# Sums of squares on ScalarE, and the first loads and conversions pinned in order of need, in a one-core hybrid encoder layer

## The chip, the cores and the metric

The kernel runs on 1 core of one Trainium2 chip. The metric is the device time of one execution in microseconds (us). An execution has five engines that run their own instruction queues: PE (TensorE, matmuls), DVE (VectorE), ACT (ScalarE), POOL (GpSimd) and SP (SyncE, which issues most of the DMAs). A difference of under 0.5% is about what a measurement of this kernel cannot tell from none.

## The reference

One encoder layer on 256 tokens of width 1024, all in float32. What matters here is its beginning:

```python
h = _rmsnorm(x, g_mix)                      # x * rsqrt(mean(x*x) + 1e-6) * g
rq, rk, rv, rg, nq, nk, nv, xq, gates = jnp.split(h @ w_in, split_points, axis=-1)
mem_n = _rmsnorm(mem, g_mem)                # 256 memory tokens of width 1024
mk, mv = jnp.split(mem_n @ w_mem_kv, 2, axis=-1)
...
lg_f = jax.nn.log_sigmoid(ret_decay_fwd)    # 4 heads; the same for bwd
...
x = x + (g_ret * y_ret + g_na * y_na + g_xa * y_xa) @ w_out
x = x + _hierarchical_moe(_rmsnorm(x, g_ffn), ...)   # 16 experts, 100 MB of weights
return _rmsnorm(x, g_final)
```

`nv`, `xq`, `nq` are 512 columns each of `h @ w_in` (values and queries of the neighbourhood attention, queries of the attention to the memory); `mk` and `mv` are the memory's keys and values.

## The kernel before, in words

**Products in three passes.** Every float32 product is made of three fp32r matmuls: each operand is split into a high part and the rest, and high x high, rest x high and high x rest are summed in PSUM (L261 to L263, L278 to L280 and L294 to L296). So a weight needs two steps before PE may use it: ACT casts the raw tile to its high part (`conv`, L126), DVE subtracts that from the raw tile (L127). A `unit` is one load of 1 MiB (L119) and two such conversions. Four raw tiles (`raw_tags`) and five tiles for the split halves (`hl_tags`) go round, so a load waits for the DVE of an earlier unit and a cast for the PE of an earlier unit.

**The norm is applied late.** The matmuls run on `x` times the gain only (`gained`, L235 and L237: ACT makes the high part, DVE the rest). The factor 1/rms of each token is worked out beside them: `squares` (L205 to L212) squares and sums the transposed tokens on POOL in eight instructions, `tokens` (L214 to L223) sums over partitions with two tiny matmuls into a PSUM tile (L219), DVE adds the epsilon (L221), POOL raises to the power -0.5 (L222). That gives `col`, one factor per token on the partition axis. `row_of` (L225 to L231) turns it into a row, by two DVE multiplications into the tile of the squares (L227), a matmul against ones (L228) and a copy from PSUM (L230). `pair_T` and `pair_N` multiply a result by the row or the column and split it.

**The order of the start.** A hand-ordered block (L243 to L263) first runs 17 transposes on PE, then, for each quarter `q` of the 1024 rows, `squares`, `gained`, the weight conversions (L256, L257) and 12 matmuls of `nv`, 48 in all, of 512 columns each. Then `tokens` for x, and `xq`, the row of x, `nq`, the memory's gains and squares, `tokens` for the memory, `mk`, the memory's row and `mv`, in this order on PE. `xq`, `nq` and `mk` are 96 matmuls of 256 columns each, `mv` 48 of 512. Outside of the hand-ordered blocks a scheduler sets the order on each engine by its own costs; an instruction in `keep_in_program_order` stays where the program has it. Each engine takes its instructions strictly in the order that results.

**Later.** The retention's decays come in by a load of 8 numbers (L385), and a chain of small DVE instructions works out their log-sigmoid (L421 to L439). Then attention, retention, the gates, the output product, and from about 330 us the 16 experts, whose weights are read straight from HBM.

Of the kernel before, what the change touches and what calls it, by code (L numbers as in the profile page):

```python
# [30 lines left out]
def hybrid_encoder_kernel(  # L31
# [101 lines left out]

# [70 lines left out]

    def squares(src, sq, q, pin=lambda i: i):  # L205
        dst = slice(2, 4) if q else slice(0, 2)
        ks = slice(2 * q, 2 * q + 2)
        pin(G.tensor_tensor(sq[:, dst], src[:, ks], src[:, ks], op=ALU.mult))
        if q:
            pin(G.tensor_tensor(sq[:, :2], sq[:, :2], sq[:, 2:4], op=ALU.add))  # L210
        if q == 3:
            pin(G.tensor_tensor(sq[:, 0], sq[:, 0], sq[:, 1], op=ALU.add))  # L212

    def tokens(sq):  # L214
        ones_f = tmp([P, P])
# [5 lines left out]
        V.tensor_scalar(col, pt[:, 2, :2], 1.0 / D, 1e-6, op0=ALU.mult, op1=ALU.add)  # L221
        tc.keep_in_program_order(G.tensor_tensor(col, col, nhalf[:, :2], op=ALU.pow))  # L222
        return col, pt, ones_f  # L223

    def row_of(tag, sq, col, pt, ones_f):  # L225
# [157 lines left out]
    mv_hi, mv_lo = pair_N("C1", proj_N(units(w_mem_kv[0], 512, D), memT_hi, memT_lo), col_m)  # L383
# [1013 lines left out]
```

## Time and profile before

| what | value |
|---|---|
| median of 3 runs | 555.55 us (554.69 to 557.27) |
| the profiled execution, its own time | 555.26 us |
| its span, first to last instruction | 553.4 us |
| PE busy | 533.1 us, 96% |
| DVE busy | 271.6 us, 49% |
| ACT busy | 225.7 us, 41% |
| POOL busy | 53.5 us, 10% |
| moved by DMA | 158.87 MB, mean 287 GB/s |

The span is 1.86 us shorter than the execution's own time. A line of the windows view gives, for a stretch of the span, each engine's busy time and number of instructions, the granted TensorE clock (1.00 is full), the DMA engines' busy share and their GB/s. A line of the timeline is one instruction, or several alike that follow each other (xN): start, duration, engine, line, operation, what it writes and reads, and in brackets how long its engine sat idle before it and what ended that. A matmul's duration is longer than the distance to the next one, since matmuls overlap; how fast PE goes is read from the distance between starts.

### The profile page before, as it was taken

The numbers are of one execution on the slowest core, as the hardware profiler recorded it, in microseconds if no ns is written. First come the engines' busy times: TensorE is split into PE (matmuls) and PEld (weight loads), VectorE is DVE, ScalarE is ACT, GpSimd is POOL, SyncE is SP. The second block draws the span as 40 slices with busy tenths as digits, with TensorE's granted clock in tenths as the row PEclk, the third lists the DMA queues.
The fourth block names the chain that finished last, engine by engine and source line by source line (L and its number), as shares of the span: only waits on it lengthen the run. The fifth ranks groups of instructions, "written<-read, shape, count | busy, mean of one in ns | idle before, by whom it ended". The sixth has DMA issues, their size and how long they took to land.

```text
span 553.4 us, 7530 instructions
## 1 busy us (share of the span) xinstructions
PE 533.1 (96%) x2916; PEld 363.6 (66%) x2916; DVE 271.6 (49%) x462; ACT 225.7 (41%) x372; POOL 53.5 (10%) x61
## 2 busy tenths in 40 slices
PE   8898999999999999999999999999999999999990
PEld 6798899987778888888888863353435343533440
DVE  6989759997647758565466271030112101211122
ACT  6653455877674555545435251121111111211132
POOL 5246601030000040000000000000000000000000
PEclk9899999999999999999999999999999999999996
DMA  8973998144443699648994598999999999999942
GB/s 290 386 238 113 226 262 208 54 152 153 152 146 125 202 346 349 216 152 324 374 345 172 218 366 319 417 406 415 408 415 408 410 411 408 416 405 416 407 172 81
DMA packets 80969, 158.87 MB, mean 287 GB/s; under 512 B 4496, under 2 KB 18864, under 8 KB 80928
## 3 DMA queue, kind: packets, MB, share of 16 engines
q1 hardware_dynamic: 79152, 154.68, 75.6%
q0 software_dynamic: 1488, 3.60, 3.7%
q8 instruction: 25, 0.41, 0.3%
q14 instruction: 16, 0.13, 0.1%
q10 hardware_dynamic: 288, 0.05, 0.0%
HBM read 157.27 MB, written 1.05 MB: 286 GB/s over the span
## 4 chain that ended last, share of the span: by engine, by line
PE 90%; POOL 2%; issue 2%; DVE 1%; DMA 1%; ACT 1%; SPq 0%; ACTq 0%
PE b L1163 20%; PE pj L294 9%; PE pj L295 9%; PE pj L296 9%; PE b L1182 9%; PE b L1095 3%; PE pj L278 3%; PE pj L280 3%; PE pj L279 3%; PE pj L1220 3%; PE at L330 1%; PE pj L846 1%; PE pj L848 1%; PE pj L847 1%; PE b L1193 1%
## 5 line engine op out<-in xcount | busy, mean ns | idle before, releaser
L127 DVE TENSOR_TENSOR h<-r,h 128x1024 fp32r<-128x1024 f32 x58 | 73.1, 1269 | 32.5 <-ACT h L126 32.1
L126 ACT CAST h<-r 128x1024 fp32r<-128x1024 f32 x58 | 59.9, 1048 | 26.8 <-PE pj L296 12.3
L294 PE MATMUL pj<-h,A 128*128 128x512 f32 x160 | 63.1, 394 | 0.0
L295 PE MATMUL pj<-h,A 128*128 128x512 f32 x160 | 62.5, 391 | 0.0
L296 PE MATMUL pj<-h,A 128*128 128x512 f32 x160 | 62.4, 390 | 0.0
L1171 DVE TENSOR_TENSOR gs<-gs,b 64x512 f32<-64x512 f32 x16 | 11.1, 691 | 87.1 <-ACT gs L1170 87.1
L278 PE MATMUL pj<-A,h 128*128 128x256 f32 x160 | 45.6, 285 | 0.0
L280 PE MATMUL pj<-A,h 128*128 128x256 f32 x160 | 45.5, 284 | 0.0
L279 PE MATMUL pj<-A,h 128*128 128x256 f32 x160 | 45.4, 284 | 0.0
L294 PEld LDWEIGHTS pj<-h,A 128*128 128x128 f32 x160 | 30.0, 188 | 7.1 <-issue 0.8
L296 PEld LDWEIGHTS pj<-h,A 128*128 128x128 f32 x160 | 30.0, 188 | 6.7 <-issue 0.4
L295 PEld LDWEIGHTS pj<-h,A 128*128 128x128 f32 x160 | 30.1, 188 | 6.2 <-DVE h L127 0.4
L1202 DVE SCALAR_TENSOR_TENSOR os<-b,c,os 128x512 fp32r<-128x512 f32 x16 | 12.0, 750 | 42.2 <-ACT os L1201 41.4
L280 PEld LDWEIGHTS pj<-A,h 128*128 128x128 f32 x160 | 30.7, 192 | 0.1
L279 PEld LDWEIGHTS pj<-A,h 128*128 128x128 f32 x160 | 30.7, 192 | 0.0
L278 PEld LDWEIGHTS pj<-A,h 128*128 128x128 f32 x160 | 30.7, 192 | 0.0
L1170 ACT ACTIVATE gs<-b 64x512 f32<-64x512 f32 x16 | 9.4, 589 | 51.8 <-PE b L1163 51.8
L1201 ACT ACTIVATE os<-b,c 128x512 fp32r<-128x512 f32 x16 | 11.0, 688 | 40.9 <-PE b L1182 39.9
L127 DVE TENSOR_TENSOR h<-G,h 128x1024 fp32r<-128x1024 f32 x18 | 22.0, 1232 | 7.1 <-ACT h L126 6.9
L1163 PE MATMUL b<-h,C 128*64 128x512 f32 x104 | 24.0, 592 | 0.0
L126 ACT CAST h<-G 128x1024 fp32r<-128x1024 f32 x18 | 18.9, 1049 | 11.5 <-PE pj L296 9.0
L1244 POOL TENSOR_TENSOR rstd<-var,nhalf 128x1 f32<-128x1 f32 x2 | 1.1, 542 | 219.2 <-DVE var L1243 219.2
(342 smaller groups left out, 1106.7 us busy)
## 6 DMA issues: line engine op xcount, KB each, us to landing
r<-in_w_in_dram SPq DMA_DIRECT2D x21, 1024.0 KB, 5.2
h<-in_w_exp_down_dram SPq DMA_DIRECT2D x10, 1024.0 KB, 11.5
h<-in_w_exp_gate_dram SPq DMA_DIRECT2D x13, 512.0 KB, 10.9
h<-in_w_exp_up_dram SPq DMA_DIRECT2D x13, 512.0 KB, 11.0
r<-in_w_exp_down_dram SPq DMA_DIRECT2D x6, 1024.0 KB, 11.4
G<-in_w_in_dram SPq DMA_DIRECT2D x5, 1024.0 KB, 9.5
A<-in_w_exp_down_dram SPq DMA_DIRECT2D x5, 1024.0 KB, 11.4
r<-in_w_exp_gate_dram SPq DMA_DIRECT2D x9, 512.0 KB, 10.2
```

What stands on the lines that cost most here:

```text
L126: A.copy(hi, part)
L127: V.tensor_sub(lo, part, hi.bitcast(F32))
L278: PE.matmul(pt, whi[:, cs], thi[:, k], start=k == 0, stop=False)
L279: PE.matmul(pt, whi[:, cs], tlo[:, k], start=False, stop=False)
L280: PE.matmul(pt, wlo[:, cs], thi[:, k], start=False, stop=k == kn - 1)
L294: PE.matmul(pts[a], thi[:, kk, ts], whi, start=first, stop=False)
L295: PE.matmul(pts[a], thi[:, kk, ts], wlo, start=False, stop=False)
L296: PE.matmul(pts[a], tlo[:, kk, ts], whi, start=False, stop=last)
L1095: PE.matmul(pts[u][:, j], x[:, a, ks], pd[:, a].rearrange("p e s -> p (e s)"), start=first and j + a == 0, stop=not first and j + a == 2,)
L1163: PE.matmul(pt[c * 64 : c * 64 + 64], xg[:, k, p % 2 * 2 + i], w[:, 2 * c + j], start=k == 0, stop=k == KT - 1)
L1182: PE.matmul(pts[n][i * 64 : i * 64 + 64], hh[:, 2 * u + k], ws[i][1][:, k, ns], start=u + k == 0, stop=u + k == 2)
L1220: PE.matmul(acc[a][n], q[:, a * P : (a + 1) * P], os[n][:, i], start=False, stop=last and i == 1)
```

## The change

The sums of squares leave POOL. For x, a second copy of x in its natural layout (1 MiB, tokens on partitions) is loaded after the weights of `xq`; ACT squares it and sums along the row in the same instruction (`accum_out`), which gives the per-token sum without a matmul. For the memory, ACT squares the transposed tokens in two instructions, POOL adds the pieces in three (1024, 512 and 256 columns), and the two tiny matmuls stand between the two halves of `mk` (`mid`), not ahead of it. `col` and row keep their form, but the multiplications of the row write a tile of their own, and the ones are made once. The weights of `xq` are loaded in four pieces in place of two; those of `nq`, `mk` and `mv` are converted at places that the program fixes. The decays are loaded at the very start, on ACT's DMA queue, and four DVE instructions that stood where the scheduler put them (the two multiplications of the rotary tables, and the two that read the decays) are pinned.

```diff
+    dec = cp.tile([P, 8], F32, name="dec")
+    A.dma_start(dec, decay.partition_broadcast(P))
...
-        pin(G.tensor_tensor(sq[:, dst], src[:, ks], src[:, ks], op=ALU.mult))
-        if q:
-            pin(G.tensor_tensor(sq[:, :2], sq[:, :2], sq[:, 2:4], op=ALU.add))
-        if q == 3:
-            pin(G.tensor_tensor(sq[:, 0], sq[:, 0], sq[:, 1], op=ALU.add))
+    def squares(src, sq):
+        pin = tc.keep_in_program_order
+        for h in range(2):
+            ks = slice(4 * h, 4 * h + 4)
+            pin(A.activation(sq[:, ks], src[:, ks], AF.Square))
+        for n in (4, 2, 1):
+            pin(G.tensor_tensor(sq[:, :n], sq[:, :n], sq[:, n : 2 * n], op=ALU.add))
...
+    def diag_of(col):
+        diag = tmp([P, T])
         for a in range(2):
-            V.tensor_scalar_mul(sq[:, 1, a * P : (a + 1) * P], ident, col[:, a : a + 1])
-        PE.matmul(pt[:, 0], ones_f, sq[:, 1], start=True, stop=True)
+            tc.keep_in_program_order(V.tensor_scalar_mul(diag[:, a * P : (a + 1) * P], ident, col[:, a : a + 1]))
+        return diag
...
-            squares(xT, sq, q)
             gained(xT, 0, hT_hi, hT_lo, ks)
...
-    col_x, *mean_x = tokens(sq)
...
+    xq_u = units_T(W, C_XQ, D, parts=2)
+    x_n = slot("F", [P, 2, D])
+    nc.sync.dma_start(x_n, x[0].rearrange("(a p) d -> p a d", p=P))
+    ms = tiny(2, tag="ms")
+    for a in range(2):
+        tc.keep_in_program_order(A.activation(x_n[:, a], x_n[:, a], AF.Square, accum_out=ms[:, a : a + 1]))
+    col_x = tiny(2, tag="col")
+    tc.keep_in_program_order(V.tensor_scalar(col_x, ms, 1.0 / D, 1e-6, op0=ALU.mult, op1=ALU.add))
+    power(col_x)
...
-    pts = proj_T(units_T(W, C_XQ, D), hT_hi, hT_lo)
-    row_x = row_of("q", sq, col_x, *mean_x)
+    pts = proj_T(xq_u, hT_hi, hT_lo)
+    nq_u = units_T(W, C_NQ, D, pin)
+    row_x = row_of("q", diag_of(col_x))
...
-    gained(memT, 1, memT_hi, memT_lo, range(KT))
+    pts = proj_T(nq_u, hT_hi, hT_lo)
+    gained(memT, 1, memT_hi, memT_lo, range(KT), pin)
     sq = slot("E1", [P, KT, T])
-    for q in range(4):
-        squares(memT, sq, q, tc.keep_in_program_order)
-    nq_hi, nq_lo = pair_T("E0", proj_T(units_T(W, C_NQ, D), hT_hi, hT_lo), row_x)
-    col_m, *mean_m = tokens(sq)
-    pts = proj_T(units_T(w_mem_kv[0], 0, D), memT_hi, memT_lo)
-    row_m = row_of("gs", sq, col_m, *mean_m)
+    mk_u = [unit(w_mem_kv[0][:, :256], 256, pin=pin)]
+    squares(memT, sq)
+    mk_u.append(unit(w_mem_kv[0][:, 256:512], 256, pin=pin))
+    nq_hi, nq_lo = pair_T("E0", pts, row_x)
+    cols = []
+    pts = proj_T(mk_u, memT_hi, memT_lo, lambda: cols.append(tokens(sq)))
+    (col_m,) = cols
+    diag_m = diag_of(col_m)
+    mv_u = units(w_mem_kv[0], 512, D, pin)
+    row_m = row_of("gs", diag_m)
...
-    dec = cp.tile([P, 8], F32, name="dec")
-    nc.sync.dma_start(dec, decay.partition_broadcast(P))
...
-    V.tensor_mul(cos, cos, row_x)
-    V.tensor_mul(sin, sin, row_x)
+    pin(V.tensor_mul(cos, cos, row_x))
+    pin(V.tensor_mul(sin, sin, row_x))
...
-    V.tensor_scalar_mul(e8, dec, -1.0)
+    pin(V.tensor_scalar_mul(e8, dec, -1.0))
...
-    V.tensor_scalar_min(lg, dec, 0.0)
+    pin(V.tensor_scalar_min(lg, dec, 0.0))
```

Three places show what moves. First, ACT between the conversions of `xq` (h on r and G of `w_in`) and the rows of the memory. Before (G_30 is the memory, E_17 a half of `nv`, h_35 to h_39 are the halves of `nq`):

```order
L126 CAST h_23_247<-G_21_242 128x1024
L235 ACTIVATE B_31_364<-G_30_362,gt 128x256 x5
L365 ACTIVATE E_17_231<-pj_127,col_228 128x512
L235 ACTIVATE B_31_364<-G_30_362,gt 128x256 x3
L126 CAST h_35_393<-r_34_391 128x1024
L126 CAST h_36_396<-r_34_391 128x1024
L126 CAST h_38_401<-r_37_399 128x1024
L126 CAST h_39_404<-r_37_399 128x1024
L126 CAST h_49_524<-r_48_522 128x1024
L301 CAST C_27_353<-t_28_354 128x512
```

Of the change (F_236 is x in its natural layout, h_26 to h_30 are the halves of `nq`, h_44 the first of `mk`):

```order
L126 CAST h_18_233<-G_16_227 128x1024
L380 ACTIVATE F_236,ms_238<-F_236 128x1024 x2
L386 ACTIVATE E_22_244<-pj_131,col_241 128x512
L126 CAST h_26_347<-r_25_345 128x1024
L126 CAST h_27_350<-r_25_345 128x1024
L126 CAST h_29_355<-r_28_353 128x1024
L126 CAST h_30_358<-r_28_353 128x1024
L313 CAST C_34_368<-t_35_369 128x512
L313 CAST C_34_368<-t_36_373 128x512
L246 ACTIVATE B_38_379<-G_37_377,gt 128x256 x8
L126 CAST h_44_498<-r_43_496 128x1024
L126 CAST h_45_501<-r_43_496 128x1024
```

The squares of x and the power behind them now stand ahead of the conversions of `nq`, and the eight gains of the memory have gone behind the split of `xq` (C_34).

Second, POOL at the memory's sums. Before (E_33 are the squares, G_30 is the memory):

```order
L208 TENSOR_TENSOR E_33_382<-G_30_362 128x512 x2
L210 TENSOR_TENSOR E_33_382<-E_33_382 128x512
L208 TENSOR_TENSOR E_33_382<-G_30_362 128x512
L210 TENSOR_TENSOR E_33_382<-E_33_382 128x512
L208 TENSOR_TENSOR E_33_382<-G_30_362 128x512
L210 TENSOR_TENSOR E_33_382<-E_33_382 128x512
L212 TENSOR_TENSOR E_33_382<-E_33_382 128x256
L222 TENSOR_TENSOR col_519<-col_519,nhalf 128x2
```

Of the change, POOL's whole start from the power of x on:

```order
L218 TENSOR_TENSOR col_241<-col_241,nhalf 128x2
L215 TENSOR_TENSOR E_42_495<-E_42_495 128x1024
L215 TENSOR_TENSOR E_42_495<-E_42_495 128x512
L215 TENSOR_TENSOR E_42_495<-E_42_495 128x256
L218 TENSOR_TENSOR col_579<-col_579,nhalf 128x2
```

The multiplications are gone from POOL, for x all of it but the power; the additions for the memory are left.

Third, DVE where the decays' chain begins. Before (t_43 is the first half of `nq`, h_52 and h_53 are halves of `mk`; 21 more of the chain follow, mixed with the next conversions):

```order
L127 TENSOR_TENSOR h_52_532<-G_51_530,h_52_532 128x1024
L302 TENSOR_TENSOR E_42_505<-t_43_506,E_42_505 128x512
L421 TENSOR_SCALAR e_71_730<-dec 128x8
L438 TENSOR_SCALAR lg<-dec 128x8
L422 TENSOR_TENSOR e_71_730<-e_71_730,dec 128x8
L425 TENSOR_SCALAR den_734<-e_71_730 128x8
L426 RECIPROCAL den_734<-den_734 128x8
```

Of the change (C_70 is the second half of `mv`, G_71 holds the cosines and sines, mx_772 belongs to the first softmax over the memory):

```order
L317 SCALAR_TENSOR_TENSOR C_70_712<-pj_663,col_579,C_70_712 128x512
L418 TENSOR_TENSOR G_71_717<-G_71_717,row_366 128x256
L419 TENSOR_TENSOR G_71_717<-G_71_717,row_366 128x256
L446 TENSOR_SCALAR e_73_724<-dec 128x8
L349 TENSOR_REDUCE mx_772<-at_759 128x4
L447 TENSOR_TENSOR e_73_724<-e_73_724,dec 128x8
L127 TENSOR_TENSOR h_110_997<-r_109_995,h_110_997 128x1024
L450 TENSOR_SCALAR den_728<-e_73_724 128x8
L350 TENSOR_SCALAR mx_772<-mx_772 128x4
L451 RECIPROCAL den_728<-den_728 128x8
```

The chain and the two multiplications of the tables by the row stand nine conversions later, inside the first softmax.

## Rows read from the trace of the kernel before

**Rows 1.** The page's first line: the span.

```profile
span 553.4 us, 7530 instructions
```

**Rows 2.** Windows: busy us (instructions) of each engine, PE clock, DMA share, GB/s.

```profile
5.30:22.90 17.60, 14.65 (x51) 10.45 (x51) 17.11 (x19) 12.47 (x22) 8.90 (x7) 0.90 1.05 370
16.80:20.10 3.30, 3.30 (x9) 2.56 (x8) 3.30 (x6) 2.14 (x3) 0.00 (x0) 0.51 1.09 387
34.80:46.80 12.00, 12.00 (x99) 11.75 (x97) 11.91 (x11) 5.00 (x6) 10.96 (x7) 1.00 0.42 126
73.40:85.00 11.60, 11.60 (x99) 11.60 (x98) 5.99 (x8) 7.59 (x17) 0.00 (x0) 1.00 0.86 275
85.00:125.00 40.00, 40.00 (x304) 36.69 (x303) 39.33 (x69) 28.21 (x56) 8.01 (x8) 1.00 0.48 133
300.00:540.00 240.00, 238.83 (x1243) 110.88 (x1242) 50.37 (x121) 50.08 (x97) 1.12 (x2) 1.00 0.96 374
```

**Rows 3.** Timeline, 11 to 24 us: start us, us, engine, what, [idle before].

```profile
11.58 2.69 DVE L237 SCALAR_TENSOR_TENSOR A<-E,gt,A 128x256 fp32r<-128x256 f32 x2
...
12.40 1.15 ACT L256 CAST h<-r 128x512 fp32r<-128x512 f32 x2
...
12.74 0.39 PE L261 MATMUL pj<-h,A 128*128 128x512 f32 x1
...
14.19 2.89 DVE L257 TENSOR_TENSOR h<-r,h 128x512 fp32r<-128x512 f32 x2
...
15.99 0.50 PE L263 MATMUL pj<-h,A 128*128 128x512 f32 x1 [2.34 <-DVE h L257]
...
17.01 0.87 DVE L237 SCALAR_TENSOR_TENSOR A<-E,gt,A 128x256 fp32r<-128x256 f32 x2
...
17.80 1.28 DVE L257 TENSOR_TENSOR h<-r,h 128x512 fp32r<-128x512 f32 x2
...
21.19 2.11 ACT L235 ACTIVATE B<-G,gt 128x256 fp32r<-128x256 f32 x5 [0.22 <-DMA G<-in_mem_t_dram]
...
22.29 0.40 PE L262 MATMUL pj<-h,A 128*128 128x512 f32 x1
...
22.52 0.39 PE L263 MATMUL pj<-h,A 128*128 128x512 f32 x1
...
22.75 0.50 PE L219 MATMUL at<-t,E 128*128 128x1 f32 x4
```

**Rows 4.** Timeline, 24 to 29 us.

```profile
24.56 0.89 POOL L222 TENSOR_TENSOR col<-col,nhalf 128x2 f32<-128x2 f32 x1 [8.03 <-DVE col L221]
...
27.27 1.99 ACT L126 CAST h<-r 128x1024 fp32r<-128x1024 f32 x2
...
28.52 1.22 DVE L127 TENSOR_TENSOR h<-r,h 128x1024 fp32r<-128x1024 f32 x1
```

**Rows 5.** Timeline of PE, 46 to 49 us.

```profile
46.41 0.28 PE L279 MATMUL pj<-A,h 128*128 128x256 f32 x1
46.53 0.28 PE L280 MATMUL pj<-A,h 128*128 128x256 f32 x1
48.57 0.61 PE L219 MATMUL at<-t,E 128*128 128x1 f32 x4 [1.75 <-POOL E L212]
```

**Rows 6.** Timeline of PE, where mv begins.

```profile
60.87 0.58 PE L294 MATMUL pj<-h,B 128*128 128x512 f32 x1
```

**Rows 7.** POOL's instructions on E: duration ns min/median/max, first and last start, form.

```profile
L210 POOL TENSOR_TENSOR E<-E x6: 1299/1490/2138, 8.0 to 45.2; 128x512 f32<-128x512 f32 x6
...
L208 POOL TENSOR_TENSOR E<-G x4: 1235/1637/2017, 35.4 to 43.3; 128x512 f32<-128x512 f32 x4
```

**Rows 8.** Timeline of DVE: the decays' chain, first and last instructions.

```profile
47.86 0.69 DVE L421 TENSOR_SCALAR e<-dec 128x8 f32<-128x8 f32 x1
...
62.47 0.17 DVE L436 TENSOR_TENSOR acc<-acc,s 128x8 f32<-128x8 f32 x1
62.67 0.17 DVE L439 SCALAR_TENSOR_TENSOR lg<-acc,lg 128x8 f32<-128x8 f32 x1
```

More of the change, by code (lines that the diff above doesn't have):

```diff
@@ L120, in load, with conv @@
         return raw
-    def conv(raw, h):
+    def conv(raw, h, pin=lambda i: i):
         n = raw.shape[1] // 2
@@ L125, in conv, with unit @@
         _, hi, lo = hl_pair(part.shape[1:])
-        A.copy(hi, part)
-        V.tensor_sub(lo, part, hi.bitcast(F32))
+        pin(A.copy(hi, part))
+        pin(V.tensor_sub(lo, part, hi.bitcast(F32)))
         return [(hi[:, k], lo[:, k]) for k in range(n)]
-    def unit(src, cols=512):
-        raw = load(src, cols)
-        return conv(raw, 0) + conv(raw, 1)
+    def unit(src, cols=512, parts=1, **kw):
+        raw = load(src, cols, parts)
+        return conv(raw, 0, **kw) + conv(raw, 1, **kw)
     plan, ready = [], []
@@ L155, in hybrid_encoder_kernel, with units, units_T @@
     idle = []
-    def units(w, c0, rows):
-        return [unit(w[r : r + 512, c0 : c0 + 512]) for r in range(0, rows, 512)]
+    def units(w, c0, rows, pin=lambda i: i):
+        return [unit(w[r : r + 512, c0 : c0 + 512], pin=pin) for r in range(0, rows, 512)]
     def units_N(w):
         return [unit(w[:, c : c + 512]) for c in (0, 512)]
-    def units_T(w, c0, rows):
+    def units_T(w, c0, rows, pin=lambda i: i, parts=1):
         cols = 512 * 512 // rows
-        return [unit(w[:, c : c + cols], cols) for c in range(c0, c0 + 512, cols)]
+        return [unit(w[:, c : c + cols], cols, parts, pin=pin) for c in range(c0, c0 + 512, cols)]
     W = w_in[0]
@@ L203, in rstd_of @@
         return r
-    def squares(src, sq, q, pin=lambda i: i):
-        dst = slice(2, 4) if q else slice(0, 2)
-        ks = slice(2 * q, 2 * q + 2)
-        pin(G.tensor_tensor(sq[:, dst], src[:, ks], src[:, ks], op=ALU.mult))
-        if q:
-            pin(G.tensor_tensor(sq[:, :2], sq[:, :2], sq[:, 2:4], op=ALU.add))
-        if q == 3:
-            pin(G.tensor_tensor(sq[:, 0], sq[:, 0], sq[:, 1], op=ALU.add))
+    ones_f = cp.tile([P, P], F32, name="ones_f")
+    V.memset(ones_f, 1.0)
+    def squares(src, sq):
[5 more added lines that the diff above has]
+            pin(G.tensor_tensor(sq[:, :n], sq[:, :n], sq[:, n : 2 * n], op=ALU.add))
@@ L214, in tokens, with power @@
+    def power(col):
+        tc.keep_in_program_order(G.tensor_tensor(col, col, nhalf[:, :2], op=ALU.pow))
     def tokens(sq):
-        ones_f = tmp([P, P])
-        V.memset(ones_f, 1.0)
-        pt = at([P, 4, 256])
+        pt = at([P, 2])
         for a in range(2):
-            PE.matmul(pt[:, 2, a : a + 1], sq[:, 0, a * P : (a + 1) * P], ones_f[:, :1], start=True, stop=True)
+            tc.keep_in_program_order(
+                PE.matmul(pt[:, a : a + 1], sq[:, 0, a * P : (a + 1) * P], ones_f[:, :1], start=True, stop=True)
+            )
@@ L220, in tokens @@
         col = tiny(2, tag="col")
[L221 to L225, printed above, removed]
-        for a in range(2):
-            V.tensor_scalar_mul(sq[:, 1, a * P : (a + 1) * P], ident, col[:, a : a + 1])
-        PE.matmul(pt[:, 0], ones_f, sq[:, 1], start=True, stop=True)
+        V.tensor_scalar(col, pt, 1.0 / D, 1e-6, op0=ALU.mult, op1=ALU.add)
@@ L229, in row_of @@
+        power(col)
+        return col
+    def diag_of(col):
+        diag = tmp([P, T])
+        for a in range(2):
+            tc.keep_in_program_order(V.tensor_scalar_mul(diag[:, a * P : (a + 1) * P], ident, col[:, a : a + 1]))
+        return diag
+    def row_of(tag, diag):
+        pt = at([P, T])
+        PE.matmul(pt, ones_f, diag, start=True, stop=True)
         row = wp.tile([P, T], F32, tag=tag, name=nm("row"))
-        V.tensor_copy(row, pt[:, 0])
+        tc.keep_in_program_order(V.tensor_copy(row, pt))
@@ L231, in row_of, with gained @@
         return row
-    def gained(src, gi, hi, lo, ks):
+    def gained(src, gi, hi, lo, ks, pin=lambda i: i):
         for k in ks:
-            A.activation(hi[:, k], src[:, k], AF.Copy, scale=gt[:, gi, k : k + 1])
+            pin(A.activation(hi[:, k], src[:, k], AF.Copy, scale=gt[:, gi, k : k + 1]))
         for k in ks:
-            V.scalar_tensor_tensor(
-                lo[:, k], src[:, k], gt[:, gi, k : k + 1], hi[:, k].bitcast(F32), op0=ALU.mult, op1=ALU.subtract
+            pin(
+                V.scalar_tensor_tensor(
+                    lo[:, k], src[:, k], gt[:, gi, k : k + 1], hi[:, k].bitcast(F32), op0=ALU.mult, op1=ALU.subtract
+                )
@@ L247, in hybrid_encoder_kernel @@
         pn = [pj([P, 512]) for _ in range(2)]
-        sq = slot("E1", [P, KT, T])
         for q in range(4):
             ks = (2 * q, 2 * q + 1)
-            squares(xT, sq, q)
             gained(xT, 0, hT_hi, hT_lo, ks)
@@ L263, in hybrid_encoder_kernel, with proj_T @@
                     PE.matmul(pn[a], hT_hi[:, k, ts], w_lo[:, k % 2], start=False, stop=k == KT - 1)
-    col_x, *mean_x = tokens(sq)
     show("hT", hT_hi.bitcast(F32))
-    def proj_T(us, thi, tlo):
+    def proj_T(us, thi, tlo, mid=None):
         pts = [pj([P, 2, 256]) for _ in range(2)]
@@ L280, in proj_T @@
                     PE.matmul(pt, wlo[:, cs], thi[:, k], start=False, stop=k == kn - 1)
+            if mid and not ui:
+                mid()
         return pts
@@ L366, in hybrid_encoder_kernel @@
     V.tensor_scalar_mul(nv[:, 1], pn[1], col_x[:, 1:2])
-    pts = proj_T(units_T(W, C_XQ, D), hT_hi, hT_lo)
-    row_x = row_of("q", sq, col_x, *mean_x)
+    pin = tc.keep_in_program_order
+    pts = proj_T(xq_u, hT_hi, hT_lo)
+    nq_u = units_T(W, C_NQ, D, pin)
+    row_x = row_of("q", diag_of(col_x))
     xq_hi, xq_lo = pair_T("C2", pts, row_x)
@@ L373, in hybrid_encoder_kernel @@
     memT_lo = slot("B1", [P, KT, T], F32R)
-    gained(memT, 1, memT_hi, memT_lo, range(KT))
+    pts = proj_T(nq_u, hT_hi, hT_lo)
+    gained(memT, 1, memT_hi, memT_lo, range(KT), pin)
     sq = slot("E1", [P, KT, T])
-    for q in range(4):
-        squares(memT, sq, q, tc.keep_in_program_order)
-    nq_hi, nq_lo = pair_T("E0", proj_T(units_T(W, C_NQ, D), hT_hi, hT_lo), row_x)
-    col_m, *mean_m = tokens(sq)
-    pts = proj_T(units_T(w_mem_kv[0], 0, D), memT_hi, memT_lo)
-    row_m = row_of("gs", sq, col_m, *mean_m)
+    mk_u = [unit(w_mem_kv[0][:, :256], 256, pin=pin)]
[8 more added lines that the diff above has]
+    row_m = row_of("gs", diag_m)
     mk_hi, mk_lo = pair_T("C0", pts, row_m)
-    mv_hi, mv_lo = pair_N("C1", proj_N(units(w_mem_kv[0], 512, D), memT_hi, memT_lo), col_m)
-    dec = cp.tile([P, 8], F32, name="dec")
-    nc.sync.dma_start(dec, decay.partition_broadcast(P))
+    mv_hi, mv_lo = pair_N("C1", proj_N(mv_u, memT_hi, memT_lo), col_m)
     tabs = slot("G1", [P, 2048])
```

## The prediction

> **What bounds the kernel now.** I read the windows first, then PE's idle notes in the timeline, then the instructions around each of them. From 48.6 us to the last expert PE never stands still for more than a us: in the experts' stretch it is busy 238.83 of 240 us [rows 2], and the 11.6 and 40 us windows ahead of it are full too. So a change to the start can only win where PE waits ahead of that, and there are two such places. In the stretch of `nv`, PE is busy 14.65 of 17.60 us [rows 2], with one pause of 2.34 us for DVE's L257 and, behind it, 3.30 us at a granted clock of 0.51, the lower of TensorE's two levels, 1.2 GHz [rows 2, 3]. Ahead of `mk`, PE waits 1.75 us for POOL's last addition of the memory's squares [rows 5]. Everything behind hangs on PE and on buffers that PE and DVE set free, so what is won at the start should come out at the end nearly whole, if DVE follows: between 85 and 125 us it is busy 39.33 of 40 us [rows 2], and has no room to catch up there.
>
> **nv: 22.75 to 17.6.** While POOL squares x, DVE's pair of L237 takes 2.69 us and the pair of L257 takes 2.89; once POOL is done they take 0.87 and 1.28 [rows 3]. The change takes POOL out of this block altogether. What is late next? ACT casts the last weights from 12.40 to 13.55 [rows 3], as it does now. DVE then keeps close behind: its last two L257 end about 14.5. PE has 24 of its 48 matmuls left at 12.74 and needs until 22.75; at the distance of 0.23 between two starts (22.29 and 22.52) they take 24 x 0.232 = 5.6 us [rows 3]. So they would end at 18.3, and since DVE is also quicker in the two quarters before, I take off another 0.7, which gives 17.6; the operands of k = 6 and 7 (13.9 to 14.5) are then needed at 14.8 and 16.2, just in time. Without the pause I expect no fall of the clock. Bounds: 17.4 if nothing is late, 19.9 if the loads and ACT, not DVE, pace the third quarter.
>
> **xq and the row of x: a new wait.** The two small matmuls of x's sum go (22.75 to 23.1, 0.34 us). The 96 matmuls of `xq` at 0.119 us (46.41 to 46.53 [rows 5]) take 11.4 us and end at 29.0. Their weights land where they do now, one load earlier in the queue than the memory; splitting them into halves only brings the first cast forward. The price is what stands behind them: x in natural layout takes the place of the memory in SP's queue, with the same 1 MiB, and the memory is there at 21.19 [rows 3]. So x is too, and ACT, which takes its work in order, holds the casts of `nq` behind it. Two squares of 1024 columns, no row of their own, I put at a cast's 1.0 each ([rows 4]: two in 1.99), to 23.2; DVE's epsilon and POOL's power, 0.15 and 0.89 [rows 4], to 24.2; the evacuation L386 0.6; four casts to 28.8. DVE's four L127 at 1.22 [rows 4] end at 30.7, and the two multiplications by the identity, half a us, at 31.2. PE reaches the row's matmul (L239), which stands 12 matmuls into `nq`, at 30.4. I count a **wait of 0.8 us**, between 0 and 2 as x lands 0.8 earlier or 1.2 later. The matmul itself 0.43, then 84 of `nq` 10.0 us: 41.6.
>
> **The memory's sums.** After the row: its copy and two products on DVE and two splits on ACT, to 34.0; eight gains at 0.42 ([rows 3]: five in 2.11), to 37.4; two casts, to 39.4, two squares, to 41.4. Then POOL adds 1024, 512 and 256 columns. An addition of 512 took 1.30 to 2.14 us, median 1.49 [rows 7]; 1792 columns are 3.5 of these, 4.6 to 7.5 us, so they end between 46.0 and 48.9. PE is through the first half of `mk` at 41.6 + 5.7 = 47.3. I take a wait of 0.5, nearer to the median than to the maximum, in the place of 1.75. Then 0.46 for the two small matmuls (48.57 to 49.03 now), 5.7 for the second half and 0.43 for the row: `mv` begins at **54.4 in place of 60.87** [rows 6], 6.4 us earlier.
>
> On this term a rule of the Trainium skill can be weighed. DVE was busy 11.91 of 12.00 us in the stretch of the memory's squares, and POOL all the same got through its instructions at 1.24 to 2.14 us each [rows 2, 7]: the two slow each other. The Trainium skill (SBUF — State Buffer, "Who interferes with whom") says that a DVE instruction with two SBUF inputs and a GpSimd one that reads SBUF contend, and that the second fully blocks until the first is done. By that rule the additions would take their own time plus DVE's beside them, and the sum would be 1.9 us worse (a rival below). By these rows, where neither stood still, I keep 0.5.
>
> **The decays and tables.** Their load moves to ACT's queue at the start, some 0.4 us of issue that lies in ACT's wait for the first data. The chain of 26 small DVE instructions at 0.20 apart (62.47 and 62.67 [rows 8]) ran from 47.86 to 62.8, where PE had its operands in hand. Now it stands, with two multiplications of 0.42, in the stretch that is 73.4 to 85 now: 5.2 + 0.8 = 6.0 us of new DVE work where 11.6 - 5.99 = 5.6 are idle [rows 2]. 0.4 don't fit, and the full 40 us that follow don't give it back. Bounds 0 (PE has slack) and 6.0 (none of the idle time can be used); I take 0.9, the 0.4 and half a us for gaps that the chain's own dependencies tear.
>
> **Sum.** 6.4 - 0.9 = 5.5 us. Against the profiled execution's own 555.26 (span 553.4 [rows 1] and 1.86 around it) this gives **549.8**. That execution lies 0.3 under the median of the runs shown.
>
> **The rivals.**
> - *Every new wait is covered*: the row's 0.8, the sums' 0.5 and the 0.9 later fall away, 547.6. For it: each is under a us, and the scheduler placed the later work; against: the new order holds ACT behind one load. 0.15.
> - *Loads and ACT pace nv*: it ends at 19.9; `xq` at 31.3, the row no longer waits, nor do the sums, `mv` begins at 55.4. 5.5 - 0.9 = 4.6, so 550.6: the row's wait was there to absorb it. 0.12.
> - *nv doesn't change at all*, DVE being slow for another reason: `mv` begins at 58.3, 553.6. The rows at 17.01 and 17.80, quick as soon as POOL stops, speak against it. 0.05.
> - *POOL is shut out while DVE works*: 4.6 us of additions plus two L127 (2.4) and two splits (1.3) end at 49.7, the wait is 2.4, 551.7. This is the rule above; the trace doesn't bear it out in full. 0.08.
> - *Slower: the decays' chain on DVE's path.* If the idle time in 73.4 to 85 is there because ACT and DMA are late, the chain can't use it, and all 6.0 us go ahead of the first softmax and of the conversions behind it. PE then waits long enough for the clock to fall as it did at 16.8, 3.30 us at half, 1.65 us. 549.8 - 0.9 + 7.65 = 556.6. It decides from a wait of 6.4 on; DVE's 39.33 of 40 speaks for it, the 5.6 idle us against. 0.05, and 0.05 for a wait of 4 to 6 us (553 to 555).
>
> **How the numbers follow.** The forecast has 0.50, with 548.7 to 551.0 as its own range. The range for 8 in 10 reaches from the covered case less the runs' spread (547.6 - 0.8) to halfway beyond the shut-out POOL (553.2): 546.8 to 553.2. Half a per cent is what a measurement here can tell, so faster means below 552.5: 0.50 + 0.15 + 0.12 + 0.08 = 0.85. Within it lie the unchanged `nv`, the partial wait and most of the chain's case: 0.13. Above 558.0 there is 0.02.
>
> **What would show it.** Right: the granted clock stays at 1.00 in 10 to 20 us, DVE's pairs that are L237 and L257 now take 0.9 and 1.3, the last matmul of `nv` ends near 17.6, PE waits about 0.8 us for the multiplications by the identity (L234 of the change) at the row's matmul (L239), under a us for POOL at the memory's two small ones (L224), and `mv` begins near 54.4. From there to the end every mark is some 5.5 to 6.4 us earlier. Wrong: an idle note of PE over 2 us in 25 to 50, or a new one between 65 and 110 with the decays' chain or a softmax's step of DVE ahead of it; or a clock under 1.00 anywhere in the first 50 us.

## The result, and the profile after

The changed kernel takes **550.07 us** (550.00 to 551.13, 4 runs) where the one before, on the same chip, takes 555.53 (554.69 to 557.27, 4 runs): a ratio of 0.9899, 95% interval [0.9876, 0.9922]. The forecast was 549.8, and faster by more than 0.5%. Two later batches gave 549.68 (ratio 0.9902 [0.9880, 0.9924]) and 550.45 (0.9896 [0.9863, 0.9929]). One further execution of the last batch took 1088.57 us and is left out. The median is right. The profiled execution is the slowest of its four (551.13 of its own, span 549.3), and in it two of the forecast's terms are not.

| | before | predicted | after | after, decays loaded late (`e1_dec_late`) |
|---|---|---|---|---|
| first cast of a weight | 4.65 | | 6.38 | 4.62 |
| `nv` ends (start of the matmul behind it) | 22.75 | 17.6 | 19.92 | 17.31 |
| PE's wait at the row of x | none | 0.8 | none | 0.3 |
| PE's wait at the memory's sums | 1.92 | 0.5 | 0.25 | 0.26 |
| `mv` begins | 60.87 | 54.4 | 56.11 | 53.73 |
| span | 553.4 | 547.9 (549.8 less 1.86) | 549.3 | 546.7 |

The two waits of PE are distances between two starts, less the 0.12 from one matmul to the next. By that measure the idle note of 1.75 in [rows 5] is 1.92 (46.53 to 48.57).

The start of `nv` in the trace of before: timeline, 4 to 6 us, ACT and PE.

```profile
4.65 0.60 ACT L256 CAST h<-r 128x512 fp32r<-128x512 f32 x1
...
5.31 0.80 PE L261 MATMUL pj<-h,A 128*128 128x512 f32 x1
```

The same of after (ACT's L267 is L256 of before, PE's L272 is L261):

```profile
6.38 1.26 ACT L267 CAST h<-r 128x512 fp32r<-128x512 f32 x2 [1.63 <-DMA r<-in_w_in_dram]
...
7.05 0.50 PE L272 MATMUL pj<-h,A 128*128 128x512 f32 x1 [2.06 <-ACT h L267]
```

DVE's pairs in the third quarter of `nv`, and the first matmuls of `xq` (L288) and of `mv` (L306):

```profile
10.32 0.88 DVE L249 SCALAR_TENSOR_TENSOR A<-E,gt,A 128x256 fp32r<-128x256 f32 x2
11.12 1.29 DVE L268 TENSOR_TENSOR h<-r,h 128x512 fp32r<-128x512 f32 x2
...
19.92 0.28 PE L288 MATMUL pj<-A,h 128*128 128x256 f32 x1
...
56.11 0.58 PE L306 MATMUL pj<-h,B 128*128 128x512 f32 x1
```

The windows of after, with the columns of [rows 2]; the second lies inside `nv`, the third holds the memory's sums, and the last is the stretch in which the lead over before is to be kept:

```profile
5.30:17.50 12.20, 10.45 (x38) 8.18 (x39) 9.27 (x16) 9.57 (x17) 0.00 (x0) 0.86 1.07 387
8.00:12.00 4.00, 4.00 (x12) 3.08 (x12) 4.00 (x9) 3.90 (x9) 0.00 (x0) 0.57 1.06 395
...
48.00:54.50 6.50, 6.41 (x54) 6.21 (x53) 5.67 (x9) 2.09 (x2) 5.20 (x7) 1.00 0.67 204
78.00:118.00 40.00, 39.92 (x309) 37.45 (x308) 37.92 (x63) 26.77 (x51) 5.61 (x6) 1.00 0.48 132
```

The pause of 2.34 us in the middle of `nv` [rows 3] is gone, POOL is idle there. In its place PE stands still for 2.06 us ahead of the first matmul, because the first weights come in late, and then goes through 8 to 12 us at a granted clock of 0.57, for the most part on the lower level of 1.2 GHz. Not all executions do the second: in the first repetition the pause was 1.58 us, the clock stayed at 1.00, `xq` began at 18.12 and the time was 549.37; in the second it was 1.87 us, the clock 0.60, `xq` began at 19.64 and the time was 550.45.

Around the memory's sums (timeline of after, 41 to 50 us; L213 are ACT's squares, L215 POOL's three additions, L127 DVE's conversions, L224 the two small matmuls):

```profile
41.09 2.00 ACT L213 ACTIVATE E<-G 128x1024 f32<-128x1024 f32 x2
...
43.16 6.34 POOL L215 TENSOR_TENSOR E<-E 128x1024 f32<-128x1024 f32 x3 [19.14 <-ACT E L213]
...
44.36 4.55 DVE L127 TENSOR_TENSOR h<-G,h 128x1024 fp32r<-128x1024 f32 x2
...
49.56 0.61 PE L224 MATMUL at<-ones_f,E 128*128 128x1 f32 x4
```

PE's last matmul ahead of the small ones starts at 49.19, so the wait has shrunk from 1.92 us to 0.25.

### The profile page after: what moved, and what is told of

It reads as the page before. It is cut to its first block, busy times and chain, and to the rows that moved or that the text cites. A ratio compares the mean times of both kernels' runs of the same rounds, so it can differ in the third digit from the quotient of the medians.

```text
span 549.3 us, 7517 instructions
## 1 busy us (share of the span) xinstructions
PE 531.6 (97%) x2912; PEld 363.5 (66%) x2912; DVE 263.8 (48%) x461; ACT 229.3 (42%) x378; POOL 37.2 (7%) x48
## 4 chain that ended last, share of the span: by engine, by line
PE 92%; ACT 2%; DVE 2%; POOL 1%; DMA 1%; issue 1%; SPq 0%; ACTq 0%
PE b L1188 20%; PE pj L306 9%; PE pj L307 9%; PE pj L308 9%; PE b L1207 9%; PE b L1120 3%; PE pj L290 3%; PE pj L288 3%; PE pj L289 3%; PE pj L1245 3%; PE at L342 1%; PE pj L871 1%; PE pj L873 1%; PE pj L872 1%; PE b L1218 1%; PE at L343 1%
## 5 line engine op out<-in xcount | busy, mean ns | idle before, releaser
L127 DVE TENSOR_TENSOR h<-r,h 128x1024 fp32r<-128x1024 f32 x58 | 70.4, 1222 | 32.2 <-ACT h L126 31.9
L126 ACT CAST h<-r 128x1024 fp32r<-128x1024 f32 x58 | 60.2, 1047 | 27.0 <-PE pj L308 12.8
L306 PE MATMUL pj<-h,A 128*128 128x512 f32 x160 | 63.1, 395 | 0.0
L288 PE MATMUL pj<-A,h 128*128 128x256 f32 x160 | 45.7, 286 | 0.0
L306 PEld LDWEIGHTS pj<-h,A 128*128 128x128 f32 x160 | 30.0, 188 | 7.1 <-issue 0.8
L288 PEld LDWEIGHTS pj<-A,h 128*128 128x128 f32 x160 | 30.7, 192 | 0.1
L127 DVE TENSOR_TENSOR h<-G,h 128x1024 fp32r<-128x1024 f32 x18 | 24.0, 1344 | 7.8 <-ACT h L126 7.2
L1207 PE MATMUL b<-h,hh 128*64 128x512 f32 x64 | 21.3, 592 | 0.0
```

What stands on the lines that cost most here:

```text
L126: pin(A.copy(hi, part))
L127: pin(V.tensor_sub(lo, part, hi.bitcast(F32)))
L306: PE.matmul(pts[a], thi[:, kk, ts], whi, start=first, stop=False)
L1207: PE.matmul(pts[n][i * 64 : i * 64 + 64], hh[:, 2 * u + k], ws[i][1][:, k, ns], start=u + k == 0, stop=u + k == 2)
```

## The experiments

Theory: POOL beside DVE is what slowed `nv`; the memory's sums win by their place between the halves of `mk`; and the early load of the decays gives part of it back. The rivals are named with each run.

**The decays loaded late** (`e1_dec_late`), where the kernel before has them, on SP's queue behind `mv`:

```diff
-    dec = cp.tile([P, 8], F32, name="dec")
-    A.dma_start(dec, decay.partition_broadcast(P))
...
     mv_hi, mv_lo = pair_N("C1", proj_N(mv_u, memT_hi, memT_lo), col_m)
+    dec = cp.tile([P, 8], F32, name="dec")
+    nc.sync.dma_start(dec, decay.partition_broadcast(P))
```

> The changed kernel, with the load of the 8 decays back on SP's queue behind mv. Theory A, that this load at the very start holds up the first weights (first cast at 6.38 us, 4.65 in the kernel before) and so costs PE 2.06 us and then the full clock: first cast near 4.7, clock 1.00 from 5 to 12 us, nv ends at 17.5 to 18.2 in place of 19.9, the row's matmul then waits some 0.7 us for DVE, and about 1.5 us are won: 548.5 against 550.07. Rival B, that the late first weights were chance in that execution or come from the other loads: first cast near 6.4 again, 550.1 within 0.4.

548.5 us (548.23 to 548.92, 5 runs), ratio to before 0.9872 [0.9853, 0.9891]. That was another batch than the result's, so it was run again beside the changed kernel:

> The changed kernel with the decays loaded late, once more, beside the changed kernel on one chip. Theory A (the early load costs 1.0 to 2.4 us at the start): 548 to 549, 0.7 to 2.0 under the changed kernel in this batch. Rival B (that difference was one between chips or executions): within 0.5 of it.

> The changed kernel again, for the comparison with e1_again: 549.4 to 550.8. PE's pause ahead of nv is 1.5 to 2.1; whether half the clock follows it decides between the upper and the lower end.

548.45 (548.10 to 548.57, 6 runs) against 550.45 (548.96 to 552.43, 5 runs): 2.0 us, and the spread is a seventh. The early load costs that much, and **this version beats both kernels**. Timeline of ACT and PE in it (L270 is the first matmul of `nv`, L286 that of `xq`, L304 that of `mv`):

```profile
4.62 0.60 ACT L265 CAST h<-r 128x512 fp32r<-128x512 f32 x1
...
5.28 0.79 PE L270 MATMUL pj<-h,A 128*128 128x512 f32 x1
...
17.31 0.28 PE L286 MATMUL pj<-A,h 128*128 128x256 f32 x1
...
53.73 0.58 PE L304 MATMUL pj<-h,B 128*128 128x512 f32 x1
```

What the load does is seen in the DMA view of 0 to 12 us, in 40 slices of 0.3 us. After:

```profile
DMA  0000002169956559879999999999999999999999
GB/s 0 0 0 0 0 2 67 38 207 337 324 145 124 138 172 285 278 229 324 331 362 403 403 396 410 403 379 399 400 406 396 403 396 389 376 417 382 403 413 369
```

With the decays late:

```profile
DMA  0000002179999999987999999999999999999999
GB/s 0 0 0 0 0 3 62 62 197 338 372 406 369 396 382 321 280 232 246 365 365 365 338 369 389 372 348 393 372 386 348 379 389 393 393 399 379 376 386 389
```

From 3.3 to 4.5 us, when the decays are on their way, the engines move 124 to 172 GB/s in place of 369 to 406 and are only half busy. The decays are 4 KB, so the lost rate is not theirs: the large loads slow down while they are on their way.

**The same load in the kernel before** (`e6_before_dec`): a second load of the decays at the start, into a tile that nothing reads.

```diff
     A.dma_start(gt.rearrange("p a b -> p (a b)"), gains)
+    dec2 = cp.tile([P, 8], F32, name="dec2")
+    A.dma_start(dec2, decay.partition_broadcast(P))
```

> The kernel before, with one thing added: a second load of the decays at the very start on ACT's queue, which nothing reads. Theory A (the small load holds up the first large ones): the first cast moves from 4.65 to 6.0 to 6.4 and PE's first matmul of nv from 5.31 to 6.7 to 7.1. The end of nv moves by less, since DVE and POOL pace it there: 0.5 to 1.5 later, 556 to 557.3. Rival B (the delay of the first cast comes from the new order of the conversions, and the load is harmless): first cast at 4.65, no change, 555.5.

562.51 (562.22 to 564.16, 4 runs), ratio 1.0125 [1.0107, 1.0143]. The first cast came at 6.00, as theory A has it, but the cost is far beyond it. In the profiled execution, the slowest, 3.0 of 9.0 us are lost before `mv` (it begins at 63.87) and the rest in the experts, where PE waits 1.1 us in all in the kernel before. Windows of `e6_before_dec`, then of before:

```profile
350.00:500.00 150.00, 150.00 (x771) 62.43 (x765) 24.98 (x47) 25.37 (x47) 0.00 (x0) 1.00 1.04 394
505.00:520.00 15.00, 12.86 (x58) 4.53 (x56) 1.38 (x2) 1.76 (x3) 0.00 (x0) 1.00 1.03 401
```

```profile
350.00:500.00 150.00, 150.00 (x776) 63.79 (x778) 24.29 (x46) 25.48 (x47) 0.00 (x0) 1.00 1.04 411
505.00:520.00 15.00, 15.00 (x74) 5.14 (x72) 2.19 (x3) 2.81 (x5) 0.00 (x0) 1.00 1.04 410
```

The same engines, as busy, move 394 GB/s in place of 411; between 505 and 520 us PE, busy throughout before, stands still for 2.1 us, most of it for loads of weights. The edit had done a second thing: its tile of 32 bytes per partition moved every tile behind it by 32 bytes. Two runs tell the two apart. `e9_before_dec64` pads the tile to 64 bytes:

```diff
     A.dma_start(gt.rearrange("p a b -> p (a b)"), gains)
+    dec2 = cp.tile([P, 16], F32, name="dec2")
+    A.dma_start(dec2[:, :8], decay.partition_broadcast(P))
```

> e6_before_dec was 6.8 us slower, of which 1.4 to 3.0 stood at the start and the rest in the experts, where its DMA rate was 393 GB/s in place of 410. Its extra tile of 32 bytes per partition had moved every tile behind it by 32 bytes. Here the same early load of the decays, unread, goes into a tile of 64 bytes per partition, so that every large tile is again at a multiple of 64. Theory A (two effects: the early load costs the start, the shift costs DMA rate): the first cast is at 6.0 to 6.4, the experts' DMA rate is 408 to 412 GB/s from 350 to 400 us, and the time is 556.5 to 559. Rival B (the early load itself, or the chip, made the experts slow): the rate stays at 390 to 396, 561 to 563.5.

`e10_shift32` keeps the tile and drops the load:

```diff
     A.dma_start(gt.rearrange("p a b -> p (a b)"), gains)
+    cp.tile([P, 8], F32, name="shift")
```

> The kernel before with a tile of 32 bytes per partition ahead of the others that nothing loads, writes or reads; no instruction differs. Theory A (the shift by 32 bytes costs DMA rate): first cast at 4.65 to 5.0 and mv begins 0 to 1 us later than before, the experts' DMA rate is 390 to 396 GB/s from 350 to 400 us and they finish 3 to 6 us later: 558.5 to 562. Rival B (the address doesn't matter): no change, 555 to 556.

562.0 (560.65 to 562.62, ratio 1.0108 [1.0074, 1.0141]) and 561.89 (561.56 to 563.03, ratio 1.0108 [1.0074, 1.0142]). The shift alone, without a load or any other instruction, costs nearly 6 us: `mv` begins only 0.47 later, and the rest is the same 394 GB/s:

```profile
350.00:500.00 150.00, 150.00 (x778) 63.67 (x776) 24.30 (x46) 25.16 (x46) 0.00 (x0) 1.00 1.04 394
505.00:520.00 15.00, 11.40 (x50) 3.87 (x48) 0.69 (x1) 1.18 (x2) 0.00 (x0) 1.00 1.03 402
```

Here theory A holds. In `e9_before_dec64` it falls: 64 bytes are slow as well, so a multiple of 64 is not enough. Its time and rate are those of rival B, but `e10_shift32`, without the load, shows that the load is not the reason. In the built programs most large tiles lie at a multiple of 512 in the kernel before and in the changed one, and at 32 or 64 past one in these three. Which multiple is needed was not tried. The changed kernel and `e1_dec_late` hold the same tiles in another order, and both move 411 GB/s, so their difference is not of this kind.

`e9_before_dec64` also shows what the late first weights do in this kernel. Timeline, ACT and PE:

```profile
5.98 1.26 ACT L258 CAST h<-r 128x512 fp32r<-128x512 f32 x2 [1.21 <-DMA r<-in_w_in_dram]
...
6.65 0.79 PE L263 MATMUL pj<-h,A 128*128 128x512 f32 x1 [1.40 <-ACT h L258]
```

PE starts 1.34 us late, and still ends `nv` at 22.67 (22.75 before) and begins `mv` at 60.79 (60.87). But the clocks differ: behind the pause of 2.05 us in `nv` this execution kept the full clock, where the kernel before fell to 0.51 [rows 2]. `e6_before_dec`, with the same load and a pause of 2.06, fell too, and ended `nv` at 24.26, 1.51 later than before. Windows behind the pause, of `e9_before_dec64` and of `e6_before_dec`:

```profile
17.50:22.70 5.20, 5.19 (x24) 4.27 (x24) 5.20 (x8) 3.28 (x5) 0.00 (x0) 1.00 1.10 348
```

```profile
17.50:21.00 3.50, 3.47 (x8) 2.81 (x9) 3.50 (x6) 1.52 (x2) 0.00 (x0) 0.51 1.10 348
```

In the medians the load costs this kernel little: 562.0 with it (`e9_before_dec64`), 561.89 without (`e10_shift32`), both with shifted tiles. That it is free there, because DVE and POOL pace `nv`, is not shown.

**The same load on ACT's queue, but behind the conversions of `nv`** (`e8_dec_act`), issued at 12.4 us:

```diff
-    dec = cp.tile([P, 8], F32, name="dec")
-    A.dma_start(dec, decay.partition_broadcast(P))
...
+    dec = cp.tile([P, 8], F32, name="dec")
+    tc.keep_in_program_order(A.dma_start(dec, decay.partition_broadcast(P)))
     show("hT", hT_hi.bitcast(F32))
```

> The changed kernel with the decays loaded on the same queue of ACT, but behind the conversions of nv in place of ahead of them, at 13 us. Theory A (only the stretch in which the load runs counts): the first cast is at 4.6 and nv ends at 17.4, as with the late load on SP's queue; the load now runs beside the weights of xq or x, and what it delays there is 0 to 1.5 us, so the row's matmul waits 0.3 to 1.5: 548.2 to 549.5. Rival B (ACT's queue is what makes it costly, wherever it stands): casts on ACT behind it are late by 1.5 us or more and PE waits for xq's weights, 549.5 to 551.

548.84 (548.21 to 550.24, 4 runs), 0.8 under the changed kernel of the same batch (549.68; 549.14 to 550.83), with overlapping ranges. The start is as with the late load, but now the second half of `xq`'s weights and x are late, and PE waits for the row. Timeline of ACT and PE (L380 squares x):

```profile
19.87 1.05 ACT L126 CAST h<-G 128x1024 fp32r<-128x1024 f32 x1 [2.15 <-DMA G<-in_w_in_dram]
...
22.33 1.06 ACT L380 ACTIVATE F<-F 128x1024 f32<-128x1024 f32 x1 [1.41 <-DMA F<-in_x_dram]
...
32.29 0.70 PE L237 MATMUL at<-t,ones_f 128*128 128x256 f32 x2 [2.00 <-DVE t L232]
```

With the late load these squares begin at 20.60 (20.00 in the repetition). So at both places tried the small load holds up the large ones, by 1.3 to 2.3 us: the first weights in five kernels, x in this one. The time is that of theory A, though the wait is longer than its 1.5; the late cast is what rival B had named, but it cost PE no wait in `xq`. The Trainium skill (DMA: Bandwidth & Descriptors, "Issuing engines are not separate DMA queues") says that loads of different engines run on the same 16 DMA engines and interleave; the traces agree: a load issued by ACT holds up loads issued by SP, here by 1.7 to 2.3 us. The same early load on SP's queue was not run, so whether ACT's queue has a part in the delay stays open.

**POOL's squares of x back** (`e2_pool_back`): the changed kernel, with the eight POOL instructions of before beside `nv`, their result unread.

```diff
+        sx = slot("E1", [P, KT, T])
         for q in range(4):
             ks = (2 * q, 2 * q + 1)
+            dst = slice(2, 4) if q else slice(0, 2)
+            G.tensor_tensor(sx[:, dst], xT[:, 2 * q : 2 * q + 2], xT[:, 2 * q : 2 * q + 2], op=ALU.mult)
+            if q:
+                G.tensor_tensor(sx[:, :2], sx[:, :2], sx[:, 2:4], op=ALU.add)
+            if q == 3:
+                G.tensor_tensor(sx[:, 0], sx[:, 0], sx[:, 1], op=ALU.add)
```

> The changed kernel, with POOL's eight squaring and adding instructions for x put back beside nv as work that nobody reads. Theory A, that they slow DVE there: DVE's pairs in nv go from 0.87 and 1.29 to over 2 us, PE pauses for over 1.5 us in nv, which ends 2 to 3 us later (22 to 23 us), and 552 to 553 us. Rival B, that DVE was slow for another reason (loads, its own order): pairs stay at 0.87 and 1.29, 550.1.

554.91 (553.52 to 555.50, 10 runs), ratio to before 0.9984 [0.9971, 0.9997]: nearly all of the gain is gone, and more than the 552 to 553 expected. DVE, timeline:

```profile
13.92 2.68 DVE L249 SCALAR_TENSOR_TENSOR A<-E,gt,A 128x256 fp32r<-128x256 f32 x2
16.52 1.81 DVE L275 TENSOR_TENSOR h<-r,h 128x512 fp32r<-128x512 f32 x2
18.25 0.87 DVE L249 SCALAR_TENSOR_TENSOR A<-E,gt,A 128x256 fp32r<-128x256 f32 x2
```

The pair is at 2.68 again, and at 0.87 as soon as POOL is through (17.18). PE pauses for 2.05 us behind it, `xq` begins at 22.87 and `mv` at 59.14, 3.0 later than after. This execution had the full clock all through `nv`; against `after_again`, which had it too (`xq` at 18.12, `mv` at 54.34), both come 4.8 later, about as the medians do.

**The small matmuls ahead of `mk`** (`e3_sums_ahead`): the memory's sums where the text of the kernel before has them. The scheduler still put 12 of the 96 matmuls of `mk` ahead of them.

```diff
-    cols = []
-    pts = proj_T(mk_u, memT_hi, memT_lo, lambda: cols.append(tokens(sq)))
-    (col_m,) = cols
+    col_m = tokens(sq)
+    pts = proj_T(mk_u, memT_hi, memT_lo)
```

> The changed kernel, with the memory's two small matmuls ahead of all of mk, as in the kernel before, in place of between its halves. Theory A, that the place carries this part (POOL's additions end at 49.5 us, the first half of mk starts at 43.2): PE waits some 6 us for POOL, loses the full clock for 3 us behind it, 555.5 to 558. Rival B, that POOL's lighter work alone removed the wait of 1.75 us: under 1 us more, 550 to 551.

557.15 (556.51 to 558.04, 10 runs), ratio 1.0017 [1.0000, 1.0033]. Timeline and window of PE:

```profile
49.15 1.01 PE L224 MATMUL at<-ones_f,E 128*128 128x1 f32 x4 [4.35 <-POOL E L215]
```

```profile
50.00:56.00 6.00, 6.00 (x29) 6.00 (x30) 1.98 (x5) 0.42 (x1) 5.56 (x9) 0.50 0.98 283
```

ACT's squares come so late that without the new place PE waits 4.35 us for the sums and then has half the clock for 6 us: the 84 matmuls left of `mk` take 12.8 us in place of 10.0. `mv` begins at 63.04, 6.9 later than after. The move of the two small matmuls carries this part.

**The memory's squares on POOL** (`e7_mem_pool`): `e1_dec_late` with POOL's eight instructions in place of `squares(memT, sq)`; the rest, the place between the halves too, as it is.

```diff
-    squares(memT, sq)
+    for q in range(4):
+        dst = slice(2, 4) if q else slice(0, 2)
+        pin(G.tensor_tensor(sq[:, dst], memT[:, 2 * q : 2 * q + 2], memT[:, 2 * q : 2 * q + 2], op=ALU.mult))
+        if q:
+            pin(G.tensor_tensor(sq[:, :2], sq[:, :2], sq[:, 2:4], op=ALU.add))
+        if q == 3:
+            pin(G.tensor_tensor(sq[:, 0], sq[:, 0], sq[:, 1], op=ALU.add))
```

> The changed kernel with the decays loaded late (as in e1_dec_late), and the memory's squares and additions on POOL in eight instructions in place of two on ACT and three on POOL; x's sums stay on ACT, and the two small matmuls between the halves of mk. Theory A (what counts in this part is the place of the sums; ACT is not short there, but POOL's eight instructions slow DVE's casts of nq and the gains beside them): POOL works for 11 to 13 us from the memory's landing on, DVE's L127 there take 1.8 to 2.5 in place of 1.2, PE waits 1 to 3 us for DVE in nq or mk, 549.5 to 552. Rival B (ScalarE's squares cost as much as they save, since ACT holds up the casts): 547.5 to 548.5, at least as fast as with ACT.

551.17 (550.68 to 551.40, 4 runs), 2.7 above the two results of `e1_dec_late`, which are of other batches; the ratios, 0.9920 [0.9902, 0.9939] against 0.9872 and 0.9861, say the same. Timeline (L401 and L403 are POOL's, L232 the multiplications by the identity, L312 the split of `xq`, L127 the casts of `mk`):

```profile
29.56 2.69 POOL L401 TENSOR_TENSOR E<-G 128x512 f32<-128x512 f32 x2 [5.61 <-DMA G<-in_mem_t_dram]
...
30.27 2.06 DVE L232 TENSOR_SCALAR t<-ident,col 128x128 f32<-128x128 f32 x2
...
33.69 1.04 POOL L401 TENSOR_TENSOR E<-G 128x512 f32<-128x512 f32 x1
...
34.96 3.13 DVE L312 TENSOR_TENSOR C<-t,C 128x512 fp32r<-128x512 f32 x2
...
43.33 2.35 DVE L127 TENSOR_TENSOR h<-r,h 128x1024 fp32r<-128x1024 f32 x2
```

Beside POOL, L232 takes 2.06 (0.48 in `e1_dec_late`) and L312 3.13 (1.29); PE waits 1.6 us for the one and 1.2 in `mk`. ScalarE's part is worth 2.7 us here.

**The decays' chain early** (`e5_both`): `e1_dec_late`, and the two DVE instructions that read the decays no longer pinned; the scheduler puts the chain some 25 DVE instructions earlier.

```diff
-    pin(V.tensor_scalar_mul(e8, dec, -1.0))
+    V.tensor_scalar_mul(e8, dec, -1.0)
...
-    pin(V.tensor_scalar_min(lg, dec, 0.0))
+    V.tensor_scalar_min(lg, dec, 0.0)
```

> As e1_dec_late, and the two DVE instructions that read the decays are left to the scheduler, which puts their chain of 26 some 25 DVE instructions earlier. Theory A, that the chain inside the first softmax costs the 0.5 us that PE loses between 88 and 118 us in the changed kernel: 0.5 us under e1_dec_late, and the lead over the kernel before stays whole from mv to 118 us. Rival B, that this loss comes from elsewhere (the order of the other instructions): the same as e1_dec_late within 0.2.

549.91 (547.91 to 551.50, 6 runs), ratio 0.9890 [0.9866, 0.9914]. Theory A falls, and so does rival B (the same as with the late chain within 0.2): of a lead of 7.0 us at `mv` 5.0 are left at the end, less than with the late chain, and PE gets new waits there (1.0 us for ACT's L356, 0.4 for DVE). The place of the chain in the change is no loss that can be won back in this way.

**The changed kernel once more** (`after_again`), the reference of three of these runs:

> The changed kernel once more, as a reference on the same chip for the three that follow. 549.5 to 551; the first cast of a weight at 6.4, PE idle for 2 us ahead of its first product of nv, and nv ends at 19.9.

## Why the prediction was right

The median came out within 0.3 us of the forecast, and that nearness is in part luck. The sum gave 5.5 us from one profiled execution to the other; the two profiled gained 4.1 of span, and 551.13 lies 1.3 above 549.8. In that execution `nv` came out later than forecast and three smaller terms better. In `after_again`, the same kernel without the fall of the clock, the terms are much nearer: `nv` ends at 18.12, `mv` begins at 54.34, and 5.9 of span are won.

```profile
54.34 0.58 PE L306 MATMUL pj<-h,B 128*128 128x512 f32 x1
```

- ***nv* to 17.6: the mechanism right, the start missed.** DVE's pairs took 0.87 to 0.89 and 1.29 to 1.34 in every quarter, and `e2_pool_back` puts the pause back. What failed is the sentence on the decays: "some 0.4 us of issue that lies in ACT's wait for the first data". I counted the issue and not the transfer. It held the first weights up by 1.7 us, and with the half clock behind that `nv` ended 2.3 later than forecast (0.5 in `after_again`, at the full clock); the clock under 1.00 that I had named as a sign of a miss was there. With the late load `nv` ends at 17.31, and 16.56 in the repetition, against the 17.6 worked out. (Before, `nv` had a second, shorter pause, 0.58 at 10.26, which the prediction passed over.)
- **The wait at the row: 0.8 predicted, none.** x landed at 20.84, close to the 21.19 of [rows 3], and the row was ready at 32.9 (its last cast, at 30.20, had itself waited 1.73 us for PE); PE, late from `nv`, came no earlier than it. Where PE is on time (`e1_dec_late` and its repetition) the wait is 0.3 and 0.7. The rival with `nv` at 19.9 had said this, with `mv` at 55.4 (56.11) and 550.6, near the profiled execution's 551.13; but it had put the delay down to the loads and ACT themselves, and without the decays ahead of them they hardly pace `nv` (17.31 and 16.56).
- **The memory's sums: 0.5 predicted, 0.25.** POOL's additions took 6.34, between my 4.6 and 7.5. Here I had weighed a rule of the Trainium skill (SBUF — State Buffer, "Who interferes with whom") and kept the lower price. By size the rule does better than I allowed: at the 1.04 us that 512 columns took in `e7_mem_pool`, 1792 columns are an estimated 3.6; with DVE's pair of 2.35 that makes 6.0, near the 6.34. The two times nearly add up, and DVE's pair stretches as well, to 4.55. The wait stays small because the small matmuls stand behind a half of `mk`: ahead of it they waited 4.35 (`e3_sums_ahead`).
- **`mv` 6.4 earlier: 4.76,** nearly the sum of these: 2.83 at `nv` (5.15 predicted), 0.34 of small matmuls, and 1.67 at the memory's sums.
- **The later loss: 0.9 predicted, 0.6.** The lead of 4.76 at `mv` is 4.1 at the end. The chain ran inside the first softmax as expected (69.67 to 78.79), and no single wait of PE is named there. Counted matmul by matmul from the end, the lead is still 4.77 where the kernel before is at 104 us, and 4.26 where it is at 123: most of the loss comes some 20 us behind the chain. `e5_both` did not win it back, so what takes it stays open.

The upper end of the range, 553.2, does not follow from its words: halfway from 551.7 to the next rival's 553.6 is 552.65. The result lies far inside either. The rival on the slow side (the chain on DVE's path) did not occur: between 60 and 130 us PE waits for nothing that the trace names.

## What to carry to other kernels

Count what a moved load does to the loads it now runs beside, not only its issue: a transfer of 4 KB to 128 partitions cost the large ones 1.3 to 2.3 us at two places. It cost the changed kernel 2.0 us, and hardly anything in the medians of a kernel in which `nv` waited for other engines as well. Where two engines slow each other, as DVE and POOL do here (a pair of DVE 0.87 alone, 2.68 beside POOL), give the helper's work to a third, and put whoever needs it behind work that is at hand. And when an edit adds or resizes a tile, compare the DMA rate of a distant stretch before the time is read as the edit's own.

## What was not expected

- **The small load's cost.** The dip at 3.3 to 4.5 us (43 to 124 GB/s in the lowest slice) is there in each of the kernels with the early load that were looked at, and in none of those without. Why the large loads slow down for it stays open.
- **Addresses and the DMA rate.** 32 or 64 bytes of shift in nearly all large tiles take the rate in the experts from 411 to 394 GB/s, 4%, at the same busy share of the DMA engines, and the kernel's time up by about 1%. No instruction differs (`e10_shift32`).
- **A pause and the clock.** PE idled for 1.58 us ahead of `nv` with no effect on the clock in one execution, and for 1.87 and 2.06 with a clock of 0.60 and 0.57 in 8 to 12 us in two others of the same kernel. The length alone does not decide it: in `e3_sums_ahead`, with the same start, 1.57 us were followed by 0.57, and the pauses of 2.05 us in `nv` in `e2_pool_back` and `e9_before_dec64` by the full clock. This fits the changed kernel's spread of a few us, which the version with the late load, without the pause, does not have; that it explains the spread is argued from these few profiled executions.
